# Attention stage of a hybrid diffusion block: TensorE's order left to the scheduler, and the value products at highest priority with the last copied key tile first

## The chip, the cores and the metric

The kernel runs on one core of a Trainium2 chip. The metric is the device time of one launch in microseconds (us), lower is better; three runs of the kernel before gave 3588.5, 3594.65 and 3597.61 us, with the median 3594.65 us. One execution was also taken with the hardware profiler; its own time was 3600.45 us, and its span from the first to the last instruction 3598.6 us.

Engines are named as in the profile: PE is TensorE (matrix products and transposes), PEld its weight load, DVE is VectorE, ACT is ScalarE, POOL is GpSimd, SP is the engine that starts the DMAs. Each engine works through its own queue strictly in order; an instruction that waits holds back all that stand behind it on that engine.

## What is computed

One layer of a hybrid backbone on 2048 latent tokens and 256 context tokens, width 1024: a modulated RMSNorm, one input projection, two mixers side by side, one output projection, and a SwiGLU feed-forward with final norm. The stage that matters here runs both mixers:

```python
keys = concat([kc, kx]); vals = concat([vc, vx])          # 256 + 2048 = 2304 keys, 2 kv heads
s = einsum('bqkgd,bnkd->bkgqn', q, keys) * 64 ** -0.5     # 8 query heads of 64, in groups of 4
o = einsum('bkgqn,bnkd->bqkgd', softmax(s), vals)
# beside it, a gated linear recurrence in both directions, 4 heads of 128, chunkwise:
S = exp(b_last)[..., None] * S + einsum('bhsk,bhsv->bhkv', kc * exp(b_last - b), vc)
```

## The kernel before

The launch has five stages, one after the other on PE: the modulation vectors; the norm and input projection (to about 725 us of the span); the attention stage, in which softmax attention and the gated recurrence are interleaved (to about 1923 us); the output projection with the second norm (to about 2115 us); and the feed-forward (to the end). A scheduler places the instructions of every engine: it goes through the program with a clock of its own, keeps the written order as the priority, and puts on each engine the instruction of highest priority that it takes to be ready then. Where the code asks for it, an engine's instructions are left in the order in which they are written; in the attention stage this was asked for PE (L898 and L899, closed at L912).

**Attention** runs over 64 *pairs*: for each of 2 key heads, 16 blocks of 128 queries and 2 pairs of query heads. A pair's two heads are called `hh` 0 and 1, and its name is block, key head, pair (`14_1_0`). In the main loop (L900 to L940) the scores of the current pair are computed while the previous pair's probabilities are transposed and multiplied with the values:

- `scores(hh, i)`, L798: for one of three segments of 768 keys, four products into a PSUM buffer `s` (L812; there are two such buffers), the negative row minimum on DVE (L815, and at the third segment L819 over all three), then the exponential on ACT into `pr` (L820), which frees the buffer. After the third segment POOL rescales the first two segments in place (L827).
- `transposes(k2)`, L830: for one of nine tiles of 256 keys, four PE transposes of `pr` into a PSUM buffer `pt` (L835; two buffers, shared with `pof` below), copied to SBUF as `pf` by ACT (L841) or, for the tiles 2 and 5, by DVE (L839). `T_ORDER` (L858) takes the tiles 6, 7, 8, 0, 1, 2, 3, 4, 5, so tile 5 is copied last. There are nine `pf` buffers.
- `products()`, L843: 18 products of values and `pf`, two for each tile, summed in one PSUM buffer `av` (L848), then one copy `ot` on ACT (L852).
- `finish()`, L860: two transposes of `ot` into `pof` (L864), normalised on DVE (L870) and POOL (L872), and stored.

**The recurrence** is a generator; `other()` (L887) lets it go 4.4 steps further for each pair. A unit (L596) of 512 tokens has a product `pd` (L624), seven levels, each with a product `pa` (L635) that needs the `Q` of the level before from POOL (L659, L661), two groups of transposes `pk` (L675) that ACT copies out (L677), `psf` (L682), whose four blocks DVE adds into the running state `S` one after the other (L689), and `psb` (L694). `head_out` (L701) forms the outputs `po` (L725 to L727), which DVE reads last at L742. All of these share one PSUM buffer, so each needs the reader of the one before to be done.

As it was written out for PE, one pair reads: scores, two tiles of transposes, scores, one tile, scores, two tiles, scores, two tiles, scores, one tile, scores, one tile, with steps of the recurrence after most of these groups, and then the 18 products.

## Time and profile before

| what | value |
|---|---|
| median of three runs | 3594.65 us |
| profiled execution, own time / span | 3600.45 / 3598.6 us |
| PE busy, share of the span | 3448.8 us, 96% |
| DVE / ACT / POOL busy | 1755.5 / 1333.0 / 1450.9 us |
| attention stage, PE busy of 1166 us (757 to 1923 us) | 1072.2 us |
| entry to that stage, PE busy of 32.4 us (724.6 to 757 us) | 12.2 us |

The page of the profile gives busy times and the costliest groups of instructions; a view by windows gives each engine's busy time and the granted PE clock in a stretch of the span; a view of the waits gives for each pair of lines how long an engine sat idle until the other released it, how often, and the longest; the timeline lists instructions with their start and duration, and in brackets the idle time before them and who ended it.

### The profile page before, as it was taken

To read this page: it belongs to the slowest core of one execution; us is meant where nothing else is said; L and a number is where in the kernel's file an instruction comes from. 1 tells how busy PE (TensorE), PEld (TensorE's weight loads), DVE (VectorE), ACT (ScalarE), POOL (GpSimd) and SP (SyncE) were. 2 spreads that over 40 slices of the span, in tenths; PEclk is the share of its full clock that TensorE was granted. 3 is DMA by queue.
4 is the path that set the end of the run, shared out by engine and by line. 5 is a ranking of instruction groups with operands and counts; after the bars stand their busy time and mean duration, and the time that the engine had idled before them with its cause. 6 is when DMAs were issued, how large, how long until landed. Compare 5 with 4: busy or idle time off the path is not lost. (4 is left out here: it accounts for less than half of the span.)

```text
span 3598.6 us, 51540 instructions
## 1 busy us (share of the span) xinstructions
PE 3448.8 (96%) x20116; PEld 2878.4 (80%) x20116; DVE 1755.5 (49%) x2996; ACT 1333.0 (37%) x2747; POOL 1450.9 (40%) x1272
## 2 busy tenths in 40 slices
PE   8999999979999899999999999999999999999999
PEld 5999887967777777777777878888888888888887
DVE  6445655077666777666664553223224423223235
ACT  4322222166767667767653231111111311111112
POOL 4322222077767758858742132222223421221223
PEclk9999999989999999999999999999999999999999
DMA  7244655321121121111014531111112511111112
GB/s 234 91 144 133 182 158 167 98 82 31 37 62 34 34 73 39 34 46 43 17 52 156 214 120 47 47 47 47 47 48 70 211 53 41 53 48 41 59 41 88
DMA packets 279972, 294.02 MB, mean 82 GB/s; under 512 B 23120, under 2 KB 241200, under 8 KB 278448
## 3 DMA queue, kind: packets, MB, share of 16 engines
q1 hardware_dynamic: 279728, 290.73, 25.9%
q8 instruction: 158, 2.59, 0.3%
q14 instruction: 86, 0.70, 0.1%
HBM read 208.86 MB, written 81.81 MB: 81 GB/s over the span
## 5 line engine op out<-in xcount | busy, mean ns | idle before, releaser
L827 POOL TENSOR_TENSOR pr<-pr,fac 128x768 f32<-128x768 f32 x256 | 374.1, 1482 | 220.1 <-ACT fac L823 104.0
L815 DVE TENSOR_REDUCE neg<-s 128x1 f32<-128x768 f32 x384 | 365.3, 954 | 197.8 <-PE s L812 197.2
L1089 POOL TENSOR_TENSOR gl<-gs,gh 128x1024 fp32r<-128x1024 f32 x88 | 212.1, 2411 | 500.6 <-ACT gh L1088 500.5
L812 PE MATMUL s<-K,qs 128*128 128x512 f32 (+1 forms) x1536 | 372.0, 365 | 34.6 <-ACT pr L820 32.3
L1116 DVE TENSOR_TENSOR sa<-pg,sa 128x512 f32<-128x512 f32 x88 | 60.9, 692 | 682.1 <-PE pg L1109 660.7
L820 ACT ACTIVATE pr<-s,neg 128x768 f32<-128x768 f32 x384 | 348.8, 908 | 80.6 <-DVE neg L819 45.4
L812 PEld LDWEIGHTS s<-K,qs 128*128 128x128 f32 x1536 | 264.6, 192 | 106.1 <-ACT pr L820 45.6
L835 PE MATMUL pt<-identr,pr 128*128 128x128 f32 x2304 | 321.0, 275 | 8.2 <-DVE oo L870 4.0
L1149 DVE TENSOR_TENSOR yy<-yy,pd 128x512 f32<-128x512 f32 x320 | 216.6, 685 | 207.7 <-PE pd L1144 207.3
L1099 POOL TENSOR_TENSOR dl<-ds,dh 128x1024 fp32r<-128x1024 f32 x44 | 108.1, 2458 | 501.5 <-ACT dh L1098 477.2
L841 ACT ACTIVATE pf<-pt 128x512 f32<-128x512 f32 x448 | 257.1, 601 | 113.9 <-PE pt L835 111.8
L1109 PE MATMUL pg<-h2h,gh 128*128 128x512 f32 x704 | 280.0, 398 | 0.0
L1109 PE MATMUL pg<-h2l,gh 128*128 128x512 f32 x704 | 279.2, 397 | 0.0
L1109 PE MATMUL pg<-h2lr,gh 128*128 128x512 f32 x704 | 279.1, 396 | 0.0
L1109 PE MATMUL pg<-h2hr,gl 128*128 128x512 f32 x704 | 279.0, 396 | 0.0
L1109 PE MATMUL pg<-h2hr,gh 128*128 128x512 f32 x704 | 279.0, 396 | 0.0
L1109 PE MATMUL pg<-h2h,gl 128*128 128x512 f32 x704 | 278.9, 397 | 0.0
L835 PEld LDWEIGHTS pt<-identr,pr 128*128 128x128 f32 x2304 | 262.4, 141 | 17.3 <-ACT pf L841 7.2
L1144 PE MATMUL pd<-dl,hh 128*128 128x512 f32 x704 | 274.4, 390 | 0.0
L1144 PE MATMUL pd<-dh,hl 128*128 128x512 f32 x704 | 274.3, 390 | 0.0
L1144 PE MATMUL pd<-dh,hh 128*128 128x512 f32 x704 | 274.2, 389 | 0.0
L848 PE MATMUL av<-pf,V 128*64 128x256 f32 x2304 | 266.2, 385 | 7.0 <-DVE pf L839 7.0
(251 smaller groups left out, 7578.5 us busy)
## 6 DMA issues: line engine op xcount, KB each, us to landing
gs<-in_w_gu_dram SPq DMA_DIRECT2D x88, 512.0 KB
wm<-in_w_mod_dram SPq DMA_DIRECT2D x24, 1024.0 KB
ds<-in_w_down_dram SPq DMA_DIRECT2D x44, 512.0 KB
s_q<-sq SPq DMA_DIRECT2D x128, 128.0 KB
qs<-s_q SPq DMA_DIRECT2D x32, 512.0 KB
ws<-in_w_in_dram SPq DMA_DIRECT2D x9, 1024.0 KB
xt<-in_x_dram SPq DMA_DIRECT2D x16, 512.0 KB
s_f<-ft SPq DMA_DIRECT2D x16, 512.0 KB
```

The lines of the kernel that those rows point to most:

```text
L812: nc.tensor.matmul(s[:, o:o + w], self.qs[:, hh, self.item[2], half, :], self.kv[0][:, k0 + o:k0 + o + w], start=(half == 0), stop=(half = ...
L815: nc.vector.tensor_reduce(neg[:, i:i + 1], s[:, :n], axis=AX.X, op=ALU.min)
L820: nc.scalar.activation(pr[:, k0:k0 + n], s[:, :n], AF.Exp, bias=neg[:, m:m + 1], scale=-1.0, accum_out=self.ls[:, hh, i:i + 1])
L827: nc.gpsimd.tensor_tensor(pj, pj, self.fac[:, hh, j:j + 1].to_broadcast([P, SW]), op=ALU.mult)
L835: nc.tensor.transpose(pt[:, (2 * i + hh) * P:(2 * i + hh + 1) * P], self.prs[hh][:, (2 * k2 + i) * P:(2 * k2 + i + 1) * P], ident)
L841: nc.scalar.activation(pf, pt, AF.Copy)
L848: nc.tensor.matmul(self.av[i * 64:(i + 1) * 64], self.kv[1][:, 2 * k2 + i, :], self.pf[k2][:, i * 256:(i + 1) * 256], start=(n == 0), stop ...
L1089: nc.gpsimd.tensor_tensor(wl, ws, f32v(wh), op=ALU.subtract)
L1099: nc.gpsimd.tensor_tensor(dl, ws, f32v(dh), op=ALU.subtract)
L1109: nc.tensor.matmul(p, gws[ab][wi][:, k, :], h2[hf][xi][:, k, :], start=(k == 0 and i == 0), stop=(k == KT - 1 and i == 2))
L1144: nc.tensor.matmul(pd, l[:, ts_], r[:, cs], start=(i == 0), stop=(i == len(mm) - 1))
L1149: nc.vector.tensor_tensor(ys[j][:, cs], ys[j][:, cs], pd, op=ALU.add)
```

## The change

Three things change, all in the attention stage. PE's order there is no longer the written one: the scheduler places PE's instructions as it does the other engines'. The 18 products of a pair are put at the highest priority. And they go through the tiles in the reverse of `T_ORDER`, from the last copied (5) to the first (6). No instruction is added or removed. Lines between the new `with` and the removed `border` stand two further down than before, and those behind `border.close()` one line up; so L848 before is L850 now, and L864 is L866.

```diff
             def products(self):
 
                 self.av = ps_av.tile([P, 256], F32, tag="av", name=f"av{self.nm}")
-                for n, k2 in enumerate(T_ORDER):
-                    for i in range(2):
-                        nc.tensor.matmul(self.av[i * 64:(i + 1) * 64], self.kv[1][:, 2 * k2 + i, :],
-                                         self.pf[k2][:, i * 256:(i + 1) * 256],
-                                         start=(n == 0), stop=(n == len(T_ORDER) - 1))
+
+                with tc.high_priority():
+                    for n, k2 in enumerate(T_ORDER[::-1]):
+                        for i in range(2):
+                            nc.tensor.matmul(self.av[i * 64:(i + 1) * 64], self.kv[1][:, 2 * k2 + i, :],
+                                             self.pf[k2][:, i * 256:(i + 1) * 256],
+                                             start=(n == 0), stop=(n == len(T_ORDER) - 1))
...
-        border = ExitStack()
-        border.enter_context(tc.manual_schedule(engines={mybir.EngineType.PE}))
...
-                border.close()
```

What this does to the order shows at three places on PE. In the rows, a tile's name is followed by the pair's, and where it has several, by the segment ahead (`s0` to `s2`) or the key tile behind; `x2` stands for two such instructions; a line of three dots leaves out rows that repeat the two above them.

First, the products of pair `14_1_0`. Before, they follow the transposes of tile 5 directly, go from tile 6 to tile 5, and the next pair's scores come behind them:

```order
L835 MATMUL pt14_1_0_5_20552<-identr_91,pr14_1_0_1_20271 128x128
L848 MATMUL av14_1_0_20562<-pf14_1_0_6_20378,V1_14347 64x256 x2
L848 MATMUL av14_1_0_20562<-pf14_1_0_7_20385,V1_14347 64x256 x2
L848 MATMUL av14_1_0_20562<-pf14_1_0_8_20431,V1_14347 64x256 x2
L848 MATMUL av14_1_0_20562<-pf14_1_0_0_20463,V1_14347 64x256 x2
L848 MATMUL av14_1_0_20562<-pf14_1_0_1_20470,V1_14347 64x256 x2
L848 MATMUL av14_1_0_20562<-pf14_1_0_2_20518,V1_14347 64x256 x2
L848 MATMUL av14_1_0_20562<-pf14_1_0_3_20525,V1_14347 64x256 x2
L848 MATMUL av14_1_0_20562<-pf14_1_0_4_20539,V1_14347 64x256 x2
L848 MATMUL av14_1_0_20562<-pf14_1_0_5_20557,V1_14347 64x256 x2
L812 MATMUL s0_15_1_0_0_20589<-K1_14346,qs15_1_20583 128x512 x2
```

Now the following pair's first tile of transposes (`pt14_1_1_6`) and a segment of scores of the pair after that stand between:

```order
L835 MATMUL pt14_1_0_5_20550<-identr_91,pr14_1_0_1_20269 128x128
L835 MATMUL pt14_1_1_6_20594<-identr_91,pr14_1_1_0_20362 128x128
L835 MATMUL pt14_1_1_6_20594<-identr_91,pr14_1_1_1_20502 128x128
...
L812 MATMUL s1_15_1_0_0_20640<-K1_14344,qs15_1_20581 128x512 x2
L812 MATMUL s1_15_1_0_0_20640<-K1_14344,qs15_1_20581 128x256 x2
L850 MATMUL av14_1_0_20560<-pf14_1_0_5_20555,V1_14345 64x256 x2
L850 MATMUL av14_1_0_20560<-pf14_1_0_4_20537,V1_14345 64x256 x2
L850 MATMUL av14_1_0_20560<-pf14_1_0_3_20523,V1_14345 64x256 x2
```

The products moved behind work of the two following pairs, and their first one reads the tile that is copied last.

Second, three tiles of transposes of pair `14_0_1`, where before a segment of scores stood behind the first of them:

```order
L835 MATMUL pt14_0_1_1_14013<-identr_91,pr14_0_1_0_13726 128x128
L835 MATMUL pt14_0_1_1_14013<-identr_91,pr14_0_1_1_13823 128x128
...
L812 MATMUL s0_15_0_0_1_14030<-K0_7827,qs15_0_13940 128x512 x2
L812 MATMUL s0_15_0_0_1_14030<-K0_7827,qs15_0_13940 128x256 x2
L835 MATMUL pt14_0_1_2_14037<-identr_91,pr14_0_1_0_13726 128x128
L835 MATMUL pt14_0_1_2_14037<-identr_91,pr14_0_1_1_13823 128x128
...
L835 MATMUL pt14_0_1_3_14044<-identr_91,pr14_0_1_0_13726 128x128
L835 MATMUL pt14_0_1_3_14044<-identr_91,pr14_0_1_1_13823 128x128
```

Now they stand in a row, with the two buffers as before:

```order
L812 MATMUL s2_15_0_0_1_14095<-K0_7825,qs15_0_13938 128x256 x2
L835 MATMUL pt14_0_1_1_14011<-identr_91,pr14_0_1_0_13724 128x128
L835 MATMUL pt14_0_1_1_14011<-identr_91,pr14_0_1_1_13821 128x128
...
L835 MATMUL pt14_0_1_2_14035<-identr_91,pr14_0_1_0_13724 128x128
L835 MATMUL pt14_0_1_2_14035<-identr_91,pr14_0_1_1_13821 128x128
...
L835 MATMUL pt14_0_1_3_14042<-identr_91,pr14_0_1_0_13724 128x128
L835 MATMUL pt14_0_1_3_14042<-identr_91,pr14_0_1_1_13821 128x128
```

The scores moved ahead of the three tiles.

Third, the entry to the stage. Before, the recurrence's first product `pd01` stands behind the first three segments of scores of pair `0_0_0`:

```order
L812 MATMUL s2_0_0_0_0_7860<-K0_7827,qs0_0_7831 128x512 x2
L812 MATMUL s2_0_0_0_0_7860<-K0_7827,qs0_0_7831 128x256 x2
L624 MATMUL pd01_7885<-q01_7879,kk01_7881 128x128 x4
L812 MATMUL s0_0_0_0_1_7893<-K0_7827,qs0_0_7831 128x512 x2
L812 MATMUL s0_0_0_0_1_7893<-K0_7827,qs0_0_7831 128x256 x2
L812 MATMUL s1_0_0_0_1_7908<-K0_7827,qs0_0_7831 128x512 x2
```

Now six more segments and the transposes of the tiles 6, 7 and 8 are ahead of it:

```order
L812 MATMUL s2_0_0_1_0_8003<-K0_7825,qs0_0_7829 128x512 x2
L812 MATMUL s2_0_0_1_0_8003<-K0_7825,qs0_0_7829 128x256 x2
L835 MATMUL pt0_0_0_8_7980<-identr_91,pr0_0_0_0_7833 128x128
L835 MATMUL pt0_0_0_8_7980<-identr_91,pr0_0_0_1_7889 128x128
...
L835 MATMUL pt0_0_0_0_8014<-identr_91,pr0_0_0_0_7833 128x128
L624 MATMUL pd01_7883<-q01_7877,kk01_7879 128x128 x4
L812 MATMUL s0_0_0_1_1_8038<-K0_7825,qs0_0_7829 128x512 x2
```

The scheduler's places for the other engines' instructions follow PE's new order within the stage; the projection ahead of it and the feed-forward behind it keep theirs.

## The prediction

> **What bounds the kernel now.** The page's head and its busy times come first, then busy time by windows, here the entry to the attention stage, the rest of that stage, and the feed-forward (columns: window, length, busy time and count of PE, PEld, DVE, ACT and POOL, granted clock, DMA share, GB/s).

> ```profile
> span 3598.6 us, 51540 instructions
> PE 3448.8 (96%) x20116; PEld 2878.4 (80%) x20116; DVE 1755.5 (49%) x2996; ACT 1333.0 (37%) x2747; POOL 1450.9 (40%) x1272
> ```
> ```profile
> 724.60:757.00 32.40, 12.16 (x47) 10.08 (x45) 23.14 (x32) 13.46 (x31) 18.75 (x19) 0.63 0.57 165
> 757.00:1923.00 1166.00, 1072.19 (x8102) 892.87 (x8102) 791.92 (x1332) 794.57 (x1803) 833.34 (x889) 0.99 0.16 46
> 2200.00:3600.00 1400.00, 1389.87 (x5995) 1127.32 (x5993) 473.73 (x569) 245.20 (x352) 349.93 (x158) 1.00 0.20 62
> ```

> PE is the bound everywhere: 96% of the span, and 1072.19 of 1166 us even in the stage that changes, where DVE, ACT and POOL are at 68 to 71%. The change neither adds nor removes an instruction, so PE's work stays. What can move is its idle time: 1166 - 1072.19 = 93.8 us in the stage and 32.4 - 12.16 = 20.2 us at its entry, 114 us in all. That is the ceiling of any gain; a loss has no such ceiling. The view of PE's waits in the stage says what the idle time was for (us in total, times, longest).

> ```profile
> PE s L812 <- ACT pr L820: 32.3, 35, 7.9
> PE pa L635 <- POOL Q L661: 15.5, 13, 3.4
> PE pd L624 <- DVE T L666: 12.9, 1, 12.9
> PE pa L635 <- DVE S L689: 8.6, 7, 1.5
> PE av L848 <- DVE pf L839: 7.0, 2, 5.5
> PE psb L694 <- DVE S L689: 6.0, 5, 1.3
> PE po L725 <- DVE o L742: 4.8, 3, 2.3
> PE pt L835 <- ACT pf L841: 2.6, 7, 0.9
> ```

> They are many small waits for a single buffer or result to come round. For each such round I compare the time that the other engines need with the PE work that stands between its two ends in the order, before and now. PE work is priced by this piece of the timeline (start, duration), from each start to the next:

> ```profile
> 1400.46 0.96 PE L812 MATMUL s<-K,qs 128*128 128x512 f32 x4 [0.22 <-ACT pr L820]
> 1401.27 0.60 PE L835 MATMUL pt<-identr,pr 128*128 128x128 f32 x4
> 1401.70 1.06 PE L635 MATMUL pa<-Q,M 128*128 128x128 f32 x8
> 1402.69 4.11 PE L848 MATMUL av<-pf,V 128*64 128x256 f32 x36
> 1406.72 0.96 PE L812 MATMUL s<-K,qs 128*128 128x512 f32 x4
> ```

> A segment of scores is 0.81 us, a tile of transposes 0.43, a recurrence product about 0.9 (0.99 with its hand-over), a pair's products 4.03. The other engines' parts, from the groups by line (mean ns behind the busy time):

> ```profile
> L815 DVE TENSOR_REDUCE neg<-s 128x1 f32<-128x768 f32 x384 | 365.3, 954 | 197.8 <-PE s L812 197.2
> L820 ACT ACTIVATE pr<-s,neg 128x768 f32<-128x768 f32 x384 | 348.8, 908 | 80.6 <-DVE neg L819 45.4
> L841 ACT ACTIVATE pf<-pt 128x512 f32<-128x512 f32 x448 | 257.1, 601 | 113.9 <-PE pt L835 111.8
> L839 DVE COPY pf<-pt 128x512 f32<-128x512 f32 x128 | 87.1, 681 | 2.7 <-PE pt L835 2.7
> ```

> **What the new order saves.** *Entry.* Before, `pd` holds PE's queue until POOL has formed its operand:

> ```profile
> 743.05 1.79 POOL L618 TENSOR_TENSOR kk<-M,C 128x512 f32<-128x512 f32 x1
> 744.89 2.07 PE L624 MATMUL pd<-q,kk 128*128 128x128 f32 x8 [12.91 <-DVE T L666]
> ```

> Now six segments and three tiles stand ahead of it, 6 x 0.81 + 3 x 0.43 = 6.1 us of work that fits into the 12.9. Saved 6.1; bounds 0 (DVE and ACT too late for them) and 12.9. *Levels of the recurrence.* Between successive `pa` of a unit there were under 2 us of PE work at 11 of 96 places, now at 2; 15.5 x 9/11 = 12.7 (bounds 0 and 15.5). *State adds.* Behind `psf`, DVE's four adds queue among its other work:

> ```profile
> 919.89 1.16 PE L682 MATMUL psf<-V,kt 128*128 128x128 f32 x8 [0.82 <-DVE S L689]
> ...
> 923.91 1.16 PE L694 MATMUL psb<-V,kt 128*128 128x128 f32 x8 [1.29 <-DVE S L689]
> ```

> Behind `psf` there stood under 2 us of PE work at 12 of 20 places, now at 5; (8.6 + 6.0) x 7/12 = 8.5 (bounds 0 and 14.6). *Outputs.* Behind `po`, the least PE work was 3.1 us, twice, with waits of up to 2.3; so 5.4 are needed. Now the two shortest are 4.7 and 4.8, short by 1.4 together: 4.8 - 1.4 = 3.4 (bounds 0 and 4.8). Together **30.7 us**.

> **What it costs.** *Scores.* A segment waits for the buffer of the segment two before, so for one minimum and one exponential: 0.95 + 0.91 = 1.86 us at least, more with other work queued. Of the 32.3 us, 7.9 and 3.6 are two single waits behind a stalled DVE (below); 20.8 are ordinary. The PE work that is short of 2.5 us sums over the 382 places to 17.9 before, near the 20.8 measured, and to 27.3 now; 20.8 x (27.3/17.9 - 1) = 10.9. Ends: 4.7, the growth at 1.86 us, and 25.4, where the first transposes of a pair also wait for its last exponential at 2.65 us; their time I count as the same as the scores'. *Transposes.* Two buffers, freed by a copy of 0.60 or 0.68. Now 31 of 638 places, before 1, leave under 1 us. A copy that starts at once frees the buffer after 0.7 us: the shortfall grows by 5.5; with 1.2, by 16.0. I take 1.0, since an exponential often stands ahead of the copy on ACT: 14.2 - 0.6 = 13.6. *Products.* Tile 5 was read last, 3.6 us into the products; now their first instruction waits for it and all of PE with it. From its transposes to the end of its copy two cases read:

> ```profile
> 766.56 0.60 PE L835 MATMUL pt<-identr,pr 128*128 128x128 f32 x4
> ...
> 768.49 0.68 DVE L839 COPY pf<-pt 128x512 f32<-128x512 f32 x1
> ```
> ```profile
> 1491.40 0.60 PE L835 MATMUL pt<-identr,pr 128*128 128x128 f32 x4
> ...
> 1492.47 0.68 DVE L839 COPY pf<-pt 128x512 f32<-128x512 f32 x1
> ```

> 769.17 - 767.16 = 2.0 and 1493.15 - 1492.00 = 1.15 us. I take 1.5. The work that now stands between is shorter than that at 33 of 64 pairs, by 14.4 us in sum; 1.3 at 0.75, 33.4 at 2.0. *The recurrence's one buffer.* Now 26 of 223 places, before none, leave under 1 us for the reader; at 1.0 us this lacks 7.1 (1.7 at 0.75, 20.6 more than before at 1.5). Together 10.9 + 13.6 + 14.4 + 7.1 = **46.0 us**.

> **The sum.** 46.0 - 30.7 = +15.3 us. The profiled execution took 3600.45 us, 1.85 beyond its span, so 3615.75 for its like; it lies 5.8 above the median of 3594.65, and from there the forecast is **3610.0 us**, slower by 0.4%. The ends: 13.2 - 47.8 = -34.6 gives 3560, and 95.4 - 0 gives 3690. Behind the stage nothing is hidden or laid bare: the windows show the feed-forward at 99% of PE, and its order stays.

> **Rivals.** *The waits only go (faster).* The scheduler sees the recurrence's latencies, which the written order ignored; if each new short place costs only its bare copy or reduction, the losses are 4.7 + 5.5 + 1.3 + 1.7 = 13.2 against 30.7: -17.5, 3577 us. For it: POOL and DVE waits of 15.5, 8.6 and 6.0 really were of the written order. Against it: ACT and DVE are near 70% busy, so a copy seldom starts at once. It decides from losses under half of mine. *Nothing to win (same).* Scores come no faster than two buffers allow, and idle time only moves from one wait to another, within 0.3%, 3595 us. For it: PE's work is unchanged at 92% of the stage. *The change doesn't do what it says.* The products have the highest priority and yet stand later: before, at most 0.9 us of other work came between tile 5 and them in 61 of 64 pairs, now over 1 us in 53. Priority cannot start them before their first operand, so it buys nothing beyond what the order shows; this is inside the sum. *More stalls of DVE (slower still).* Some DVE instructions took far longer than their kind, and PE waited behind them:

> ```profile
> 849.64 8.88 DVE L666 TENSOR_TENSOR T<-F 128x512 f32<-128x512 f32 x1 [1.27 <-POOL Q L661]
> ...
> 1210.02 9.45 DVE L666 TENSOR_TENSOR T<-F 128x512 f32<-128x512 f32 x1 [0.56 <-POOL Q L661]
> ...
> 1781.72 6.26 DVE L865 TENSOR_TENSOR ls<-ls,fac 128x4 f32<-128x4 f32 x1 [1.67 <-ACT fac L823]
> ```
> ```profile
> 860.04 1.12 PE L848 MATMUL av<-pf,V 128*64 128x256 f32 x4 [5.47 <-DVE pf L839]
> ...
> 1222.03 1.65 PE L812 MATMUL s<-K,qs 128*128 128x512 f32 x4 [7.91 <-ACT pr L820]
> ...
> 1790.31 1.65 PE L812 MATMUL s<-K,qs 128*128 128x512 f32 x4 [3.61 <-ACT pr L820]
> ```

> During the second of them POOL's timeline has no pause, for twelve instructions, and DVE comes free as POOL does:

> ```profile
> 1209.91 0.77 POOL L647 TENSOR_TENSOR M<-M,T 128x256 f32<-128x256 f32 x1
> ...
> 1218.23 0.69 POOL L650 TENSOR_TENSOR C<-M,T 128x256 f32<-128x256 f32 x1
> 1222.42 0.63 POOL L650 TENSOR_TENSOR C<-M,T 128x256 f32<-128x256 f32 x1 [3.49 <-ACT M L653]
> ```

> Three such stalls cost PE 5.5 + 7.9 + 3.6 = 17.0 us. The new order puts DVE and POOL side by side anew; twice as many give 3627 us, none gives back 17. [...]

> **How the numbers follow.** Forecast, slower by 0.3 to 0.9%: 0.36. More stalls, or products that wait at the upper bound, 3627 to 3658: 0.15. Same: 0.21. Faster: 0.28. A measurement of this kernel tells about 0.3% from no change. So faster 0.28, same 0.21, slower 0.51. The likeliest case's own range is 3605 to 3627. For 8 in 10 the range must hold most of the faster case and of the stalls: 3566 to 3658, a little inside the ends 3560 and 3690, which need every term at its bound.

> **What would show it.** Right: waits of `av` for DVE's `pf` rise from 7.0 to about 20 us (less if no stall falls there), of `pt` for `pf` from 2.6 to about 16, of `s` for `pr` to some 40; waits of `pa` for `Q` and of `pa` and `psb` for `S` fall under half; the 12.9 us of `pd` shrink; PE's idle time of 114 us becomes about 129. Wrong: if PE's idle time falls, the short places cost their bare minimum; if one wait grows to tens of us that no term names, the order has made a new chain.

## The result and the profile after

The changed kernel took **3611.37 us** (median of 9 runs, 3599.96 to 3618.32), the kernel before 3594.65 us beside it (9 runs, 3581.90 to 3603.96). The ratio is 1.0045, with a 95% interval of 1.0025 to 1.0065: slower by some 17 us. The forecast was 3610.0 us. The number was met by luck: the experiments show that two large errors of its working cancelled.

The profiled execution of the changed kernel took 3615.77 us. The head of its page and its busy times:

```profile
span 3614.0 us, 51483 instructions
PE 3464.2 (96%) x20116; PEld 2886.0 (80%) x20116; DVE 1753.4 (49%) x2996; ACT 1331.8 (37%) x2747; POOL 1450.5 (40%) x1272
```

Span less PE's busy time is 3614.0 - 3464.2 = 149.8 us of idle time; before, it was 3598.6 - 3448.8 = 149.8 as well. **The idle time did not grow at all; the same 20116 products took 15.4 us longer.** The view by windows says where (entry and stage, columns as in the prediction; the granted clock is the number before the DMA share):

```profile
724.60:757.00 32.40, 21.59 (x101) 18.54 (x101) 20.54 (x39) 18.35 (x44) 18.29 (x17) 0.74 0.59 169
757.00:1923.00 1166.00, 1061.80 (x7991) 878.25 (x7989) 794.06 (x1319) 786.21 (x1785) 833.21 (x891) 0.97 0.15 45
```

At the entry PE is idle for 10.8 us in place of 20.2, in both together for 115.0 in place of 114.0 (the prediction's own sign was 129); the stage's clock is 0.97 in place of 0.99, and it has 7991 products in these 1166 us where there were 8102. The waits of PE in entry and stage (us in total, times, longest):

```profile
PE s L812 <- ACT pr L820: 31.7, 39, 5.9
PE av L850 <- DVE pf L839: 24.5, 16, 5.9
PE pk L675 <- DVE A L638: 10.8, 5, 7.8
PE pa L635 <- DVE li L870: 9.5, 3, 8.3
PE pt L835 <- ACT pf L841: 8.8, 17, 1.1
PE pa L635 <- DVE A L638: 8.1, 6, 5.8
PE pt L835 <- ACT pr L820: 5.5, 6, 2.7
PE pa L635 <- POOL Q L661: 4.6, 5, 1.8
...
PE po L725 <- DVE o L742: 0.2, 1, 0.2
```

The long list of recurrence waits of before (`pd` 12.9, `Q` 15.5, `S` 8.6 and 6.0, `o` 4.8) is nearly gone. In its place stand five single waits, of 5.8, 7.8, 8.3, 5.9 and 5.9 us, under five different names. Names mislead here: each is DVE *held* at one instruction, which takes many times as long as its work does. This is the case of the 8.3 us, in the timelines of DVE, POOL and PE (start, duration; in brackets the idle time before and who ended it):

```profile
1383.33 8.88 DVE L867 TENSOR_TENSOR ls<-ls,fac 128x4 f32<-128x4 f32 x1
1392.12 0.18 DVE L666 TENSOR_TENSOR T<-T 128x32 f32<-128x32 f32 x1
```
```profile
1383.00 0.66 POOL L661 TENSOR_TENSOR Q<-Q,T 128x256 f32<-128x256 f32 x1
1383.59 0.65 POOL L647 TENSOR_TENSOR M<-M,T 128x256 f32<-128x256 f32 x1
...
1390.87 0.69 POOL L647 TENSOR_TENSOR M<-M,T 128x256 f32<-128x256 f32 x1
1391.50 0.69 POOL L650 TENSOR_TENSOR C<-M,T 128x256 f32<-128x256 f32 x1
```
```profile
1394.02 2.05 PE L635 MATMUL pa<-Q,M 128*128 128x128 f32 x8 [8.27 <-DVE li L870]
1395.85 1.06 PE L835 MATMUL pt<-identr,pr 128*128 128x128 f32 x4
1396.85 5.19 PE L850 MATMUL av<-pf,V 128*64 128x256 f32 x36
```

The product `ls` brings the sums of a pair's segments to one scale, 128x4 numbers. It takes 8.88 us, where the 15 `ls` that took no longer than 0.25 us took 0.15 to 0.22, and ends at 1392.21, when POOL's unbroken run ends (1391.50 + 0.69 = 1392.19). `pa` then waits for a `li` (the reciprocal of the sums) that was merely queued behind it.

So long a hold is rare. Of the 64 `ls` of the changed kernel 49 took over 0.25 us, and each of these ended 0.02 to 0.03 us behind the end of a POOL instruction: 42 behind the first that ended, 5 behind the second, and only two behind the tenth and the twelfth. In 44 of the 47 short cases POOL went on without a pause, as here, where DVE is free at 922.28 us, in the middle of POOL's pair:

```profile
921.14 1.14 DVE L867 TENSOR_TENSOR ls<-ls,fac 128x4 f32<-128x4 f32 x1
```
```profile
920.79 2.89 POOL L827 TENSOR_TENSOR pr<-pr,fac 128x768 f32<-128x768 f32 x2 [1.80 <-ACT fac L823]
```

What makes a hold last over one POOL instruction or over twelve is not shown by any run here.

What follows the long wait in PE's timeline above is slow as well: `pa` 2.05 us for its usual 1.1, the transposes 1.06 for 0.6, the pair's products 5.19 for 4.11.

That second loss has a pattern. Every change of PE's granted clock in these profiles lies on a grid of 3.41 us. Cut into stretches at these borders, the windows around a wait of 2.57 us in the changed kernel read (second number: PE's busy time; third from the end: granted clock):

```profile
1429.85:1433.26 3.41, 2.85 (x20) 2.27 (x18) 3.31 (x3) 1.84 (x4) 3.41 (x4) 1.00 0.02 5
1433.26:1436.68 3.42, 1.31 (x12) 0.92 (x14) 3.04 (x7) 1.93 (x5) 1.68 (x4) 0.99 0.00 0
1436.68:1440.09 3.41, 3.41 (x18) 1.96 (x16) 0.00 (x0) 2.57 (x7) 2.29 (x3) 0.51 0.00 0
1440.09:1443.50 3.41, 3.41 (x27) 2.66 (x24) 0.57 (x1) 1.47 (x3) 1.27 (x1) 1.00 0.00 0
```

A stretch in which PE was busy for 1.31 us is followed by one at half clock, where its products take about twice as long: in the stage of the changed kernel the transposes follow each other by 0.213 us in place of 0.109 (medians). How little is too little is not a sharp border. The first of these two pairs of stretches is from e5, the second from e4 below:

```profile
1655.11:1658.52 3.41, 1.48 (x12) 1.16 (x9) 2.98 (x5) 2.10 (x5) 3.41 (x4) 1.00 0.00 0
1658.52:1661.93 3.41, 1.96 (x16) 1.59 (x18) 1.91 (x6) 1.51 (x5) 3.41 (x5) 1.00 0.00 0
```
```profile
1313.76:1317.18 3.42, 2.11 (x13) 1.28 (x12) 2.42 (x8) 3.03 (x7) 1.86 (x3) 1.00 1.16 344
1317.18:1320.59 3.41, 3.41 (x18) 1.95 (x18) 1.00 (x4) 0.60 (x1) 3.41 (x3) 0.50 0.90 367
```

Busy for 1.48 us, the clock stays; busy for 2.11, it is halved. Over the stage in all fourteen profiles, the stretch behind one at full clock stood at half clock in all 60 cases with PE busy for less than 1.4 us, in 26 of 51 cases between 1.4 and 1.85, and in 1 of 4551 above. So the border lies near half of a stretch in these profiles: a wait of some 2 us, unlucky in its place, costs another 1.7 us behind it, as an estimate (half of 3.41). In the stage, 9 stretches stood at half clock before, with 24.0 us of busy PE time, and 19 after, with 47.3; half of that is lost, 12.0 and 23.7 us. With the entry (9.4 and 13.2 us busy at half clock, 4.7 and 6.6 lost) the clock's part grew by 13.6 of the 15.4 us.

This compares one profiled execution of each kernel; e8 below has a second one of the changed kernel, with less. The mean granted clock of all the runs goes the same way: its median is 0.987 in the 9 runs of the changed kernel, and 0.990 in 18 runs of the kernel before (those beside e1 to e4). Three thousandths of 3600 us are 11 us, as an estimate, since the mean takes in idle time too.

### The profile page after: what moved, and what is told of

The parts are those of the page before. It is cut to its first block, busy times and chain, and to the rows that moved or that the text cites. A ratio compares the mean times of both kernels' runs of the same rounds, so it can differ in the third digit from the quotient of the medians.

```text
span 3614.0 us, 51483 instructions
## 1 busy us (share of the span) xinstructions
PE 3464.2 (96%) x20116; PEld 2886.0 (80%) x20116; DVE 1753.4 (49%) x2996; ACT 1331.8 (37%) x2747; POOL 1450.5 (40%) x1272
## 4 chain that ended last, share of the span: by engine, by line
PE 68%; DVE 7%; POOL 4%; ACT 2%; issue 2%; DMA 1%; SPq 0%; DVEq 0%; POOLq 0%; ACTq 0%
PE pg L1108 27%; PE pd L1143 13%; PE av L850 6%; PE y L1000 5%; PE s L812 5%; PE pt L835 4%; PE i L347 3%; DVE neg L815 2%; PE pa L635 2%; DVE T L666 2%; POOL pr L827 1%; ACT pr L820 1%; DVE ls L867 1%; POOL Q L661 1%; POOL Q L659 1%
## 5 line engine op out<-in xcount | busy, mean ns | idle before, releaser
L815 DVE TENSOR_REDUCE neg<-s 128x1 f32<-128x768 f32 x384 | 360.4, 951 | 225.6 <-PE s L812 224.5
L820 ACT ACTIVATE pr<-s,neg 128x768 f32<-128x768 f32 x384 | 346.4, 903 | 129.2 <-DVE neg L815 97.8
L812 PE MATMUL s<-K,qs 128*128 128x512 f32 (+1 forms) x1536 | 359.7, 363 | 32.1 <-ACT pr L820 31.7
L835 PE MATMUL pt<-identr,pr 128*128 128x128 f32 x2304 | 332.5, 278 | 20.5 <-ACT pf L841 8.8
L812 PEld LDWEIGHTS s<-K,qs 128*128 128x128 f32 x1536 | 262.6, 194 | 81.6 <-ACT pr L820 44.6
L835 PEld LDWEIGHTS pt<-identr,pr 128*128 128x128 f32 x2304 | 264.0, 143 | 54.4 <-issue 22.3
L850 PE MATMUL av<-pf,V 128*64 128x256 f32 x2304 | 275.2, 394 | 25.0 <-DVE pf L839 24.5
L841 ACT ACTIVATE pf<-pt 128x512 f32<-128x512 f32 x448 | 258.7, 599 | 75.9 <-PE pt L835 41.5
```

The source lines that it names most:

```text
L812: nc.tensor.matmul(s[:, o:o + w], self.qs[:, hh, self.item[2], half, :], self.kv[0][:, k0 + o:k0 + o + w], start=(half == 0), stop=(half = ...
L815: nc.vector.tensor_reduce(neg[:, i:i + 1], s[:, :n], axis=AX.X, op=ALU.min)
L820: nc.scalar.activation(pr[:, k0:k0 + n], s[:, :n], AF.Exp, bias=neg[:, m:m + 1], scale=-1.0, accum_out=self.ls[:, hh, i:i + 1])
L835: nc.tensor.transpose(pt[:, (2 * i + hh) * P:(2 * i + hh + 1) * P], self.prs[hh][:, (2 * k2 + i) * P:(2 * k2 + i + 1) * P], ident)
L841: nc.scalar.activation(pf, pt, AF.Copy)
L850: nc.tensor.matmul(self.av[i * 64:(i + 1) * 64], self.kv[1][:, 2 * k2 + i, :], self.pf[k2][:, i * 256:(i + 1) * 256], start=(n == 0), stop ...
```

## The experiments

Theory P is the prediction's largest single term: the products' first wait, now for tile 5's copy. Theory S came from the trace above: stalls of DVE beside POOL, and the half clock behind them. "Idle" is span less PE's busy time in the profiled execution, "long" the waits of PE over 5 us in the stage, with their sum. Ratios are to the kernel before, run beside each.

| run | median us | ratio, 95% interval | PE busy | idle | long |
|---|---|---|---|---|---|
| before | 3594.65 | | 3448.8 | 149.8 | 2, 13.4 |
| changed | 3611.37 | 1.0045 (1.0025 to 1.0065) | 3464.2 | 149.8 | 5, 33.7 |
| e1 scheduler's order alone | 3614.27 | 1.0055 (1.0037 to 1.0073) | 3558.5 | 55.5 | 0 |
| e2 no priority | 3621.48 | 1.0072 (1.0045 to 1.0098) | 3461.0 | 146.1 | 4, 26.5 |
| e3 written order, tile 5 first | 3642.98 | 1.0127 (1.0105 to 1.0148) | 3459.3 | 181.9 | 1, 5.1 |
| e4 changed, ls split | 3586.14 | 0.9984 (0.9972 to 0.9997) | 3451.5 | 132.2 | 3, 21.9 |
| e5 before, ls split | 3598.45 | 1.0013 (1.0000 to 1.0027) | 3453.8 | 146.4 | 1, 5.7 |
| e6 changed, ls split, T on POOL | 3549.72 | 0.9888 (0.9866 to 0.9909) | 3443.8 | 102.9 | 0 |
| e7 before, the same | 3590.25 | 0.9994 (0.9979 to 1.0009) | 3447.5 | 140.7 | 0 |
| e8 changed, again | 3611.07 | 1.0054 (1.0032 to 1.0075) | 3453.3 | 149.5 | 5, 33.7 |
| e9 changed, T on POOL | 3610.31 | 1.0040 (1.0022 to 1.0059) | 3457.0 | 150.3 | 5, 38.8 |
| e10 as e6, products forward | 3606.07 | 1.0020 (1.0007 to 1.0033) | 3550.1 | 47.8 | 0 |
| e11 as e6, third tile on DVE | 3547.51 | 0.9858 (0.9837 to 0.9878) | 3451.3 | 101.9 | 0 |
| e12 as e6, no priority | 3552.30 | 0.9873 (0.9853 to 0.9893) | 3447.5 | 100.6 | 0 |

### e1, e2, e3: one part of the change at a time

e1 against the changed kernel:

```diff
-                with tc.high_priority():
-                    for n, k2 in enumerate(T_ORDER[::-1]):
+                for n, k2 in enumerate(T_ORDER):
```

> TensorE's order is the scheduler's, as in the changed kernel, but the products go through the tiles as before (6 first, 5 last) and without raised priority. Theory P (the loss is the products' first wait, for tile 5's copy): of the changed kernel's 24.5 us of av waiting for pf, all but some 1.5 us go, and with them the half-clock time behind four waits of 2.1 to 2.6 us (4 x 1.7 = 6.8 us); 3611 - 24 = 3587 us, below the kernel before. Theory S (the loss is stalls of DVE beside POOL, 7 to 9 us each, and the half clock behind them): the stalls have nothing to do with the products, four to six of them remain, PE's waits of over 5 us sum to 25 to 40 us, and the time is 3600 to 3612 us.

It took 3614.27 us, the same as the changed kernel, and both theories missed why. PE no longer waits, 5.7 us in the stage; it is busy 94 us longer with the same products. e10 comes back to this.

e2 removes `tc.high_priority()` alone, e3 puts `T_ORDER[::-1]` into the kernel before and leaves its written order:

```diff
-                for n, k2 in enumerate(T_ORDER):
+                for n, k2 in enumerate(T_ORDER[::-1]):
```

> As the changed kernel, tile 5 first in the products, but without the raised priority. If the priority costs nothing by itself (as the prediction had it), the time is that of the changed kernel within 5 us, 3606 to 3616 us, and av waits for pf some 20 to 25 us. If the priority is what puts the products so close behind tile 5's copy, av's waits fall under 12 us and the time under 3600 us. Theory S expects no change beyond 5 us unless the number of long DVE stalls changes from five: each is worth 6 to 8 us of waiting and some 3 us of half clock.

e2: 3621.48 us (3601.98 to 3634.79), 10 us above the changed kernel and outside the 5 that were expected. Its interval overlaps that of the changed kernel, so the priority is not told from nothing; av waits 22.4 us for `pf`, and four long waits are left of five.

> The written order of the kernel before, with tile 5 first in the products and nothing else. In 61 of 64 pairs tile 5's transposes stand directly ahead of the products, so each pair waits from the end of its transposes to the end of the copy, with up to 0.9 us of other work between. Theory P's size, 1.5 us a pair, gives 64 x 1.5 = 96 us, 3690 us (1.15 us a pair: 3668; 2.0: 3723). If the clock is halved behind each wait that fills over half of a 3.41 us stretch, waits of 1.5 us leave the granted clock of the stage at 0.97 or higher, and waits of 2 us and more bring it under 0.9 and the time over 3750 us.

e3: 3642.98 us, (3642.98 - 3594.65) / 64 = 0.76 us a pair, half of the 1.5 that theory P had taken. The copy was not quicker than that: in e3's profile the time from the last transposes of tile 5 to the end of their copy is 1.16 us in the median of the 64 pairs, and 1.42 on average. But other work of PE stands between in 50 of the pairs, 0.89 us in the median of all, and the 96 us expected for 64 pairs had not taken it off. The stage's clock stayed at 0.98.

### e4, e5, e9: which instructions are held

e4 (changed kernel) and e5 (kernel before) take the second SBUF operand from one DVE instruction:

```diff
-            nc.vector.tensor_tensor(ls[:, :, :NSEG - 1], ls[:, :, :NSEG - 1], fac, op=ALU.mult)
+            for hh in range(2):
+                for j in range(NSEG - 1):
+                    lj = ls[:, hh, j:j + 1]
+                    nc.vector.tensor_scalar(lj, lj, fac[:, hh, j:j + 1], None, op0=ALU.mult)
```

> The changed kernel, with the product of ls and fac (DVE, two operands from SBUF, 128x4) written as four instructions with one SBUF operand and a per-partition factor each. Theory S: this instruction can no longer be held by POOL; the two stalls of 8.88 and 7.38 us that began at it go (PE waits of 8.3 and 5.9 us, and some 3 us of half clock behind each), and the time falls by about 20 us, to 3591 us; the new instructions take under 0.2 us each. Theory P: the time stays at 3611 us within 5, since the products still wait for tile 5.

> The kernel before (written order), with the product of ls and fac as four DVE instructions with one SBUF operand each, as in e4. Theory S: one of the three long stalls (6.26 us, a wait of 3.6 us and 1.7 us of half clock) began at this instruction, so 5 us are gained, 3590 us, less than the 25 us that the same edit gave in the changed kernel, where two stalls began at it. Rival (the four instructions are cheaper by themselves, whatever the order): the gain is 20 us or more here too, 3575 us or less.

e4 gained 25 us, to 3586.14: theory S had said 20, P none. The stalls at `ls` are gone, and so are the short holds: 233 of the 256 new instructions began beside a busy POOL, and none took over 0.22 us. Three long stalls are left, all at T. e5 gained nothing: the instructions are not cheaper by themselves, and the 5 us that S had expected did not come either. DVE was held twice, at T (8.87 and 6.46 us), and the waits behind it fell from 17.0 to 10.4 us, but PE's busy time was 5.0 us longer; whether that is more than the spread between executions (e8) stays open.

e9 is the other half, T alone on POOL:

```diff
-                nc.vector.tensor_tensor(T2, T3[:, :, 0, :], T3[:, :, 1, :], op=ALU.mult)
+                nc.gpsimd.tensor_tensor(T2, T3[:, :, 0, :], T3[:, :, 1, :], op=ALU.mult)
```

> The changed kernel with the recurrence's T products on POOL and nothing else (ls and fac stay one DVE instruction with two SBUF operands). Theory S: the three stalls that began at T go (PE waits of 5.8, 7.9 and 5.9 us and some 8 us of half clock), those at ls may stay or move with POOL's order; 3611 - 28 = 3583 us, between e4's 3586 and e6's 3550 but nearer to e4. If ls alone was the trouble, 3611 us within 5; if T alone was, 3550 us.

3610.31 us, nothing gained, where S had said 3583. The `ls`, still one instruction with two SBUF operands, is now held long more often, 12 times in place of two: between 4.2 and 12.75 us, behind 4 to 13 POOL instructions. That T makes POOL's unbroken runs longer would explain this, but it is not tested by itself. The worst of them, in the timelines of DVE, POOL and PE of e9:

```profile
866.54 12.75 DVE L867 TENSOR_TENSOR ls<-ls,fac 128x4 f32<-128x4 f32 x1
879.33 0.16 DVE L869 TENSOR_REDUCE li<-ls 128x2 f32<-128x6 f32 x1
```
```profile
864.76 2.95 POOL L827 TENSOR_TENSOR pr<-pr,fac 128x768 f32<-128x768 f32 x2
867.61 2.59 POOL L620 TENSOR_TENSOR Q<-q,F 128x512 f32<-128x512 f32 x2
...
875.32 2.95 POOL L827 TENSOR_TENSOR pr<-pr,fac 128x768 f32<-128x768 f32 x2
878.17 1.10 POOL L666 TENSOR_TENSOR T<-F 128x512 f32<-128x512 f32 x1
```
```profile
881.19 1.12 PE L850 MATMUL av<-pf,V 128*64 128x256 f32 x4 [11.81 <-DVE pf L839]
```

DVE is free at 879.29, POOL's run ends at 878.17 + 1.10 = 879.27. In 7 of the 12 cases POOL went on without a pause when DVE came free.

### e6, e7, e8: both orders without the stalls

e6 and e7 make both edits, in the changed kernel and in the kernel before; e8 is the changed kernel once more.

> The changed kernel with e4's edit, and with the recurrence's T products on POOL, so that besides the Sb chain DVE has no instruction with two SBUF operands. Theory S: no wait of PE over 5 us is left (e4 had three, 22 us, with some 8 us of half clock behind them), 3586 - 30 = 3556 us; POOL has some 55 us more to do and pa waits longer for Q, which may take back up to 15 us (3571). Rival (POOL's queue is then the bound of the recurrence): waits of pa for Q of over 30 us, 3590 us or more.

> The same two edits in the kernel before. Theory S: its three long stalls cost 17 us of waiting and some 10 us of half clock, so 3594 - 27 = 3567 us, plus what POOL's longer levels cost in the written order (pa waited 15.5 us for Q before; up to twice that). The comparison with e6 tells the orders apart without stalls: by the prediction's ordinary terms (46.0 of new short waits against 30.7 saved) e6 is 15 us slower than this; by the reading of the two profiles (9.4 us at the entry and some 7 us of short waits saved) it is about 16 us faster.

> The changed kernel once more, for a second profile. If the stalls are set by the order (theory S), the same places show again, four to six stalls of over 5 us with PE's waits of over 5 us summing to 25 to 40 us; if they fall at random, other places and another number.

e6: **3549.72 us**, 44 below the kernel before beside it (3593.70); theory S had said 3556. No wait over 5 us is left, and the stage's clock is 1.00. e7: 3590.25 us, no gain. The view by windows and the main waits of e6, then those of e7:

```profile
757.00:1923.00 1166.00, 1109.35 (x8308) 916.89 (x8307) 695.92 (x1414) 792.78 (x1801) 869.82 (x1030) 1.00 0.17 51
```
```profile
PE s L812 <- ACT pr L820: 28.7, 52, 4.0
PE pt L835 <- ACT pf L841: 9.1, 20, 1.3
PE av L850 <- DVE pf L839: 7.4, 7, 1.9
...
PE pa L635 <- POOL Q L661: 3.2, 4, 1.7
```
```profile
PE pa L635 <- POOL Q L661: 33.5, 21, 3.9
PE s L812 <- ACT pr L820: 18.4, 34, 4.1
PE pd L624 <- POOL kk L618: 14.0, 1, 14.0
```

In the written order the waits for `Q` double from 15.5 us with POOL's longer levels, which eats what the stalls had cost; the scheduler's order has put other work there, 3.2 us. So without long stalls the scheduler's order is 40 us faster, not 15 us slower as the prediction's ordinary terms would have it; 18 of these 40 are the longer waits for `Q` that T on POOL brings into the written order alone.

A rival for e6's gain is that DVE simply has less to do (1630.3 us busy in place of 1753.4). Two runs speak against it: e9 moves the same T products and gains nothing, and e11 below gives DVE some 41 us more to do and loses nothing.

e8 shows the same five stalls at the same instructions, of 7.63, 9.45, 8.87, 8.87 and 7.41 us where the first profile had 7.63, 9.44, 8.88, 8.86 and 7.38: they belong to the order, not to chance. Two rows of DVE's timeline in e8:

```profile
1199.11 9.45 DVE L666 TENSOR_TENSOR T<-F 128x512 f32<-128x512 f32 x1
1377.49 8.87 DVE L867 TENSOR_TENSOR ls<-ls,fac 128x4 f32<-128x4 f32 x1
```

Its waits are the same too (idle 149.5 us), yet PE's busy time is 10.9 us shorter (3453.3). That much one kernel varies between executions. Of the 10.9 us 7.9 are the clock's: in e8's profile 15 stretches of the stage stand at half clock where the first had 19, with 35.9 us of busy time, and 8.9 at the entry, so 22.4 us are lost where the first lost 30.3. Against the kernel before (16.7) that is 5.7 us more, not 13.6, so the clock's share in the 17 us is known no better than that. Why the same waits cost one execution more clock than another, perhaps by their place against the borders of the stretches, was not tested.

### e10, e11, e12: what the reversed products are for

All three start from e6. e10 sends the products forward and without priority (the edit of e1), e12 keeps them reversed without priority, e11 lets DVE copy a third tile:

```diff
-EV_DVE = (2, 5)
+EV_DVE = (8, 2, 5)
```

> As e6 (no instruction that POOL can hold, but the Sb chain), with the products forward and not at high priority, as in e1. There the products stood in single groups between transposes and PE was 1160 us busy of 1166 with 5.7 us of waits. Theory W (each change between the 64-column products and other products costs PE some 0.14 us, 76 us in the stage): PE stays full, so taking the stalls out gains little, 3600 to 3614 us. Theory S alone (e1 was slow for its stalls): 3550 to 3565 us, as e6.

> As e6, tile 5 first, but without the raised priority of the products: e2's question once more, without the long stalls that spread e2's times. If the priority decides nothing on the clock, the time is e6's within 5 us, 3545 to 3555 us, with av's waits for pf at 6 to 9 us. If it keeps the products together and that is worth something, PE's busy time for the same work grows and the time is 3560 us or more.

> As e6, with a third tile of nine (tile 8) copied by DVE in place of ACT: 64 copies, ACT 0.60 us each less (38 us), DVE 0.68 each more (44 us). DVE was busy for 696 of 1166 us and ACT for 793, so the waits for ACT (s for pr 28.7 us, pt for pf 9.1) should fall by a third and the time to 3538 us. Rival: DVE's copies stand ahead of the minima, the waits of s for pr grow instead, and the time is 3555 us or more.

e10 took 3606.07 us, as theory W had it, and e12 3552.30: the direction of the products alone is worth 54 us. Forward, each tile's products become ready as its copy ends, and the scheduler places them singly between other work; from tile 5 backwards, all are ready together and mostly stay in one piece. PE changes between `av` and other products 1074 times in e10's trace and 166 times in e12's. Busy times of e10's page, then of e12's:

```profile
PE 3550.1 (99%) x20116; PEld 2824.7 (79%) x20116; DVE 1649.2 (46%) x3048; ACT 1338.8 (37%) x2747; POOL 1489.2 (41%) x1412
```
```profile
PE 3447.5 (97%) x20116; PEld 2869.9 (81%) x20116; DVE 1630.2 (46%) x3048; ACT 1327.9 (37%) x2747; POOL 1486.7 (42%) x1412
```

(3550.1 - 3447.5) / (1074 - 166) = 0.113 us a change. PE's timeline of e10 shows it from start to start, and the timeline of the weight loads shows what goes with it:

```profile
1400.89 0.65 PE L848 MATMUL av<-pf,V 128*64 128x256 f32 x4
1401.48 0.66 PE L835 MATMUL pt<-identr,pr 128*128 128x128 f32 x4
```
```profile
1401.48 0.42 PEld L835 LDWEIGHTS pt<-identr,pr 128*128 128x128 f32 x4 [0.39 <-issue]
1401.86 0.76 PEld L812 LDWEIGHTS s<-K,qs 128*128 128x128 f32 x4
1402.57 0.46 PEld L835 LDWEIGHTS pt<-identr,pr 128*128 128x128 f32 x4
```

These four products of `av` take 1401.48 - 1400.89 = 0.59 us, where a pair's 36 in one piece took 4.03, 0.45 for four. The first weights of 128 columns behind `av`'s 64 begin to load at 1401.48, as the first product that uses them starts, after 0.39 us without a load; between products of the same width the loads run on (1401.48 + 0.42 = 1401.90, the next begin at 1401.86). The 0.113 us are an estimate that puts the whole difference in busy time down to the changes; what PE does at one of them was not shown.

e12's time is e6's within the intervals, so the priority decides nothing that these runs can tell. e11's 3547.51 us is not told from e6 either: the waits of `s` for `pr` fell from 28.7 to 26.8 us, not by a third. e6, e11 and e12 are all faster than the kernel before, by 1.1 to 1.4%.

## Why the prediction was right in its number and wrong in its sum

*What bounds it.* Right: PE, and its waits in this one stage. Wrong: that only idle time can move. Idle stayed at 149.8 us; PE's speed moved. A mean clock of 0.99 in the windows was read as full.

*Savings, 30.7 us forecast.* Right in kind, too small. Entry 20.2 to 10.8 us of idle, 9.4 (forecast 6.1). Levels, `Q` 15.5 to 4.6, 10.9 (12.7). State adds, 8.6 + 6.0 to 0.2, 14.4 (8.5). Outputs 4.8 to 0.2, 4.6 (3.4). Together 39.3. More was saved in small waits that no term named, all of the written order: for `kt`, for ACT's `A` and `dS`, and for `oo`, some 13 us.

*Costs, 46.0 us forecast.* Without the stalled waits: products 7.0 - 5.5 = 1.5 to 24.5 - 5.9 = 18.6, up 17.1 (14.4). Scores, behind the entry (whose waits are in the 9.4 already: 6.9 us of the 32.3 before, 10.2 of the 31.7 after): 25.4 - 7.9 - 3.6 = 13.9 to 21.5 - 5.9 = 15.6, and first transposes 0.8 to 4.9, together up 5.8 (10.9). The copies' part of the transposes, `pf` of ACT and DVE 2.6 + 0.2 to 8.8 + 1.6, up 7.6 (13.6). The one buffer: `pk` and `pa` for `A` and `li`, 2.5 to 10.8 + 9.5 + 8.1 + 1.0 less the three stalls of 7.8, 8.3 and 5.8, so 7.5, up 5.0 (7.1). Sum 35.5, so three of the four terms were too large, and the named costs did not outweigh the named savings. As a whole: without the stalled waits, PE's idle time in entry and stage was 114.0 - 17.0 = 97.0 us before and 115.0 - 33.7 = 81.3 after, 15.7 less where the forecast had 15.3 more. The one cost that came out larger, the products', is only in part the copy of tile 5: av's waits fall from 18.6 to 7.4 us in e6, where no long hold is left. The rest was DVE's queue.

*What failed* is the rival "more stalls", which the prediction priced at 17 us but left out of the forecast, with the likeliest case at no change from before. Waits behind a held DVE went from 17.0 to 33.7 us, twice as much, just as that rival said. And the clock behind the waits, 13.6 us more between the two profiles (5.7 with e8's), was in no term. These 30 us took the place of the 31 that the ordinary terms had too much: the order alone was a gain (e6 against e7). The rival "the waits only go" had that gain at 17.5 us, near the 15.7, but not by its working: its costs of 13.2 came out at 35.5, and larger savings paid for them.

*How long a hold lasts.* The prediction set POOL's timeline beside one stall, of 9.45 us over twelve POOL instructions. Most holds of the changed kernel end with the first POOL instruction that ends (42 of 49 `ls`), but not the long ones that PE waited for, which for `ls` lasted over 10 and 12 instructions, and in e9 up to 13. `ls` was held, and T three times for 7.63 to 9.44 us; the reductions from PSUM beside them were not (L815 in the changed kernel: all 384 between 0.92 and 0.96 us, 260 of them begun beside a busy POOL), and `ls` as products with one factor a partition no more (none of 256 over 0.22 us, e4).

*The rival "doesn't do what it says"* was right on the priority, as far as e2 and e12 can tell. On the reversal the prediction saw a cost only; it keeps the products together, worth 54 us in the scheduler's order (e10 against e12). This did not show in the result, as the written order had them together already.

## What to carry to other kernels

Before pricing a new order by its short waits, list the instructions that take far longer than their kind, see with which other engine's instructions they end, and give them a form that is not held, or another engine; here two such edits together turned a loss of 17 us into a gain of 44, while one of them alone gained 25 and the other nothing. Price a wait with what the clock does behind it: look at windows of the length at which the clock changes (3.41 us here), not at a stage's mean. An order that leaves no idle time can still be slow (e1, 98% busy): compare the busy time of the same work as well.
